# A hybrid encoder trunk: token norms spread by a trip through DRAM, mLSTM gates as 32 extra columns of the first value group

## The chip, the cores and the metric

The kernel runs on one core of one Trainium2 chip. The metric is device time in microseconds of one execution; lower is better. The core has five engines with in-order queues of their own: TensorE (PE in the profile; its weight loads are PEld), VectorE (DVE), ScalarE (ACT), GpSimd (POOL) and SyncE (SP), which here only issues DMAs.

## The reference

Two layers over 256 tokens of width 2048, everything in float32. What the change touches is the RMS norm ahead of every projection, and the gates of the second layer's mLSTM mixer:

```python
def rms_norm(x, g):
    y = xf * lax.rsqrt(jnp.mean(xf * xf, axis=-1, keepdims=True) + NORM_EPS)
    return (y * g)                       # one factor per token, one gain per channel
def mlstm_mixer(h, w_in, b_gate, h_norm, w_out):
    proj = h @ w_in                      # columns: q | k | v | o (2048 each) | 32 gates
    ...
    gates = proj[..., 4 * MLSTM_W:] + b_gate    # 4 kinds (i, f forward; i, f backward) x 8 heads
    h_fw = mlstm_one_direction(q, k, v, gates[0], gates[1])
    h_bw = flip(mlstm_one_direction(flip(q), flip(k), flip(v), flip(gates[2]), flip(gates[3])))
    ...                                  # sum, per-head norm, sigmoid output gate, output projection
for layer in range(2):
    h = rms_norm(x, norm_mix[layer])
    mixed = attention/pool mixer (layer 0) or mlstm_mixer (layer 1)
    x = x + mixed
    x = x + conv_ffn(rms_norm(x, norm_ffn[layer]), ...)
```

Inside a direction the forget gates are log-sigmoided and summed along the tokens, a running maximum is taken, and exp of both weighs a token-by-token matrix per head.

## The kernel before

**Precision and matmuls.** Each float32 operand is split in a high and a low part (type float32r), and a product is made of three matmuls: high x high, high x low, low x high. Weights stream from DRAM in chunks of 128 partitions x 1024 float32 (512 KB). `Stream` loads them on SP's queue into 6 buffers (`wraw`), and `split` makes the two parts: an ACT copy rounds to the high part (L87), a DVE subtraction leaves the low part (L88), into 4 buffers (`wsplit`). The split of a chunk is done two chunks ahead of its use.

**Two forms of a projection.** `stat_group` holds a weight block stationary and streams the 256 tokens (512 moving columns are the high and the low parts of the activations side by side, 256 the high ones alone); its output is channels x tokens. `mov_group` holds the activations stationary and streams weight columns; its output is tokens x channels, for each of 16 blocks of 128 input channels (`k`) 2 token halves x 3 matmuls of `width` columns. Both write tiles of the PSUM pool `mm`, which has two buffers; small products use the pool `ps` with four.

**Order.** TensorE's order is written out by hand: whatever the Python code emits first runs first (`manual_schedule`). ACT, DVE and POOL are ordered by the framework's scheduler, which follows readiness in a model of the time; an instruction without inputs can move far ahead. `Weave` puts side work between TensorE's main groups: each side task is a generator, a `yield d` asks to be continued when the estimated clock has moved on by d us, and that clock moves by `tick` after each `k` (0.645 in `stat_group`, 1.29 x width / 512 in `mov_group`). The emission, not the chip, follows this clock.

**Tiles.** A pool tile has a tag; tiles of one tag share the tag's buffers, and the framework makes a tile wait until a buffer is its own. The pool `t1p` (`ml_1`) of the mLSTM layer has one buffer a tag. Its tag `vf` holds in turn `wgf` (raw gate weights), `mvf0` (the scaled values of the first two heads, L804), `rows_a` (four rows of the gate work), and then `mvf1` and so on; `rows_b` takes the tag `at`.

**Norms.** `Norm.block` transposes the residual stream x on TensorE (`xt`), and `Norm.parts` gives gain and split (`xx`), without the per-token factor. `Norm.finish` adds up the squares, takes the inverse root (`rsqrt`, one POOL power and four small DVE steps), which gives `rcol`: tokens on partitions, 128 x 2. To have the same factors as a row on every partition, it builds two diagonal matrices `dg` (DVE, L270) and multiplies them with a matrix of ones on TensorE (`npr`), and copies the result to `R` (L275). `R` multiplies outputs that are channels x tokens: the pool channels, the FFN's up-projection (L850), mLSTM's q and k (L699). `rcol` scales outputs that are tokens x channels.

**mLSTM layer.** Per pair of heads: the values (`mov_group` of 512 columns, `mv0` to `mv3`), then q and k of each head (`stat_group`, `mq0`, `mk0`, ...), then the output gates (`mo`; for the last pair two groups of 256 columns). After `mv0` has been emitted its two halves are scaled into `mvf0` (ACT, L806) and split into `mvt0` (ACT L808, DVE L809). Then the task `gates` is added: on TensorE 16 x 2 stationary matmuls with gate weights padded to 104 rows (`gps`), emitted after the first `k` of `mq0`; then on ACT and DVE the chain that makes log-sigmoid (Abs, Exp, Ln: L665 to L667), sums (scans, L672 and L673), running maxima (L675 and L676), their sum (L677, the last use of `rows_a`) and an exp `E` (L678); the rows go to DRAM (`gd`), from where each head's `G` is spread to all partitions. 13.0 us of the estimated clock later TensorE transposes the maxima and `E` into columns (`cols`), which all heads need.

Of the kernel before, what the change touches and what calls it, by code (L numbers as in the profile page):

```python
# [9 lines left out]
F32 = mybir.dt.float32  # L10
F32R = mybir.dt.float32r
AF = mybir.ActivationFunctionType
# [4 lines left out]
P = 128  # L17
D = 2048
S = 256
KT = D // P  # L20
# [8 lines left out]
MH = 8  # L29
MD = 256  # L30
# [3 lines left out]
CH = 8  # L34
# [8 lines left out]


C_ID = 0
C_ONE = C_ID + P
C_CONV = C_ONE + P
C_PSC = C_CONV + 2 * 88 * 4
C_HN = C_PSC + 4
NC_ALL = C_HN + 16  # L50
# [14 lines left out]
class Stream:  # L65
# [6 lines left out]
        self.n_load = self.n_split = self.at = 0  # L72

    def load(self, pieces=1):
        i, n = self.n_load, CH * P // pieces
        w = self.wpool.tile([P, CH * P], F32, tag="w", name=f"w{i}")
        for c in range(0, CH * P, n):
            self.nc.sync.dma_start(w[:, c : c + n], self.srcs[i][:, c : c + n])
        self.w[i] = w, n
        self.n_load += 1  # L80

    def split(self):
        i = self.n_split
        w, n = self.w.pop(i)
        hl = self.spool.tile([P, 2, CH * P], F32R, tag="hl", name=f"hl{i}")
        for c in range(0, CH * P, n):
            self.nc.scalar.copy(hl[:, 0, c : c + n], w[:, c : c + n])  # L87
            self.nc.vector.tensor_sub(hl[:, 1, c : c + n], w[:, c : c + n], hl[:, 0, c : c + n].bitcast(F32))  # L88
        self.hl[i] = hl
        self.n_split += 1  # L90
# [60 lines left out]


@with_exitstack
def trunk(ctx: ExitStack, tc: tile.TileContext, xT, xn, gains, call, catt, cml, wgate, weights, out):
    nc = tc.nc
    v, a, g, pe = nc.vector, nc.scalar, nc.gpsimd, nc.tensor

    def pool(name, bufs, **kw):
        return ctx.enter_context(tc.tile_pool(name=name, bufs=bufs, **kw))
# [5 lines left out]
    sp = pool("wsplit", 4)  # L165
    smp = pool("small", 2)
    sm1 = pool("small1", 1)
    mmp = pool("mm", 2, space=PSUM)
    psp = pool("ps", 4, space=PSUM)

# [10 lines left out]

    wv = Weave()
    ident = cst[:, C_ID : C_ID + P]
    ones = cst[:, C_ONE : C_ONE + P]

    def gain(n, k):
        c = n * KT + k
# [2 lines left out]
    def mm(out_, lhsT, rhs, start, stop):  # L190
        pe.matmul(out_, lhsT, rhs, start=start, stop=stop, skip_group_check=True)  # L191
# [25 lines left out]
    class Norm:  # L217


        def __init__(self, n):  # L220
            self.n = n
            self.xx = actp.tile([P, KT, 2, S], F32R, tag="A", name=f"xx{n}")
            self.ss = smp.tile([P, 2, NB], F32, tag="nss", name=f"nss{n}")
            self.blocks, self.R = 0, None

        def at(self, k):

# [33 lines left out]
        def finish(self):  # L261
            n = self.n
            yield from wv.wait(lambda: self.blocks == NB)
            s2 = smp.tile([P, 2], F32, tag="nsum", name=f"nsum{n}")
            v.tensor_reduce(s2, self.ss, AX.X, ALU.add)
            self.rcol = rsqrt(s2, 2, 1.0 / D, f"n{n}")
            yield 2.5
            dg = sm1.tile([P, 2, P], F32, tag="dg", name=f"dg{n}")
            for t in range(2):
                v.tensor_scalar_mul(dg[:, t, :], ident, self.rcol[:, t : t + 1])  # L270
            yield 1.0
            pr = psp.tile([P, 512], F32, tag="ps", name=f"npr{n}")
            mm(pr[:, 0:S], ones, dg.rearrange("p a b -> p (a b)"), True, True)
            R = sm1.tile([P, S], F32, tag="R", name=f"R{n}")
            v.tensor_copy(R, pr[:, 0:S])  # L275
            self.R = R

    def stat_group(act, kts, name):
# [37 lines left out]

    def mov_group(act, name, width=512, before=None, after=None):

        ps = mmp.tile([P, 2, width], F32, tag="mm", name=name)
        per = CH * P // width  # L320
        hl = None
        for k in range(KT):
            if k % per == 0:
                before and before(k)
                hl = st.next()
                after and after(k)
            src = act(k)
            c = (k % per) * width
            for t in range(2):
                xh, xl = src[:, 0, t * P : t * P + P], src[:, 1, t * P : t * P + P]  # L330
                o = ps[:, t, :]
                first, last = k == 0 and (width == 512 or t == 0), k == KT - 1 and (width == 512 or t == 1)
                mm(o, xh, hl[:, 0, c : c + width], first, False)
                mm(o, xh, hl[:, 1, c : c + width], False, False)
                mm(o, xl, hl[:, 0, c : c + width], False, last)
            wv.tick(1.29 * width / 512)
        return ps
# [281 lines left out]
    def mlstm_layer(norm, nxt):  # L619
        with ExitStack() as es:  # L620
# [3 lines left out]
            kp, tp, t1p = lp("ml_c", 1), lp("ml_t", 2), lp("ml_1", 1)  # L624
            kc = kp.tile([P, NC_ML], F32, tag="kc", name="kml")
            a.dma_start(kc, cml)
            wgf = t1p.tile([P, KT, 4, MH], F32, tag="vf", name="wgf")
            a.dma_start(wgf.rearrange("p k c h -> p k (c h)"), wgate)

            wgp = actp.tile([P, KT, 2, P], F32R, tag="B0", name="wg")  # L630
            g.memset(wgp.bitcast(F32), 0.0)
            wg4 = wgp.rearrange("p k a (c h) -> p k a c h", c=4)[:, :, :, :, :MH]
            a.copy(wg4[:, :, 0], wgf)
            v.tensor_sub(wg4[:, :, 1], wgf, wg4[:, :, 0].bitcast(F32))
            wg = wgp[:, :, :, :NGATE]
            catb = [actp.tile([P, 8, 2, S], F32R, tag=f"B{i}", name=f"mcat{i}") for i in range(2)]

            def cat(k):
# [6 lines left out]
                [40, S], F32, tag="gd", name="gd")  # L645
            gate = []

            def gates():
                ps = psp.tile([P, 2, S], F32, tag="ps", name="gps")[:NGATE]
                for k in range(KT):  # L650
                    src = norm.xx[:, k]
                    mm(ps.rearrange("p a b -> p (a b)"), wg[:, k, 0, :], src.rearrange("p a b -> p (a b)"),
                       k == 0, False)
                    mm(ps[:, 1, :], wg[:, k, 1, :], src[:, 0, :], False, k == KT - 1)
                pre = kp.tile([NGATE, S], F32, tag="pre", name="pre")
                a.copy(pre, ps[:, 1, :])
                v.tensor_add(pre, ps[:, 0, :], pre)
                v.tensor_mul(pre, pre, norm.R[:NGATE])
                v.tensor_scalar_add(pre, pre, kc[:NGATE, M_BG : M_BG + 1])
                ra = t1p.tile([40, 4, S], F32, tag="vf", name="rows_a")  # L660
                rb = t1p.tile([40, 4, S], F32, tag="at", name="rows_b")
                la, le, ll, B, gg, M, E, on = (r[:, j, :] for r in (ra, rb) for j in range(4))
# [135 lines left out]
                    done.add(h)  # L798

            hns, done = {}, set()  # L800
            wv.add(norm.finish(), 8.0)
            for hp in range(MH // 2):
                ps = mov_group(xx, f"mv{hp}")
                vf = t1p.tile([P, 2, 512], F32, tag="vf", name=f"mvf{hp}")  # L804
                for t in range(2):
                    a.activation(vf[:, t, :], ps[:, t, :], AF.Copy, scale=norm.rcol[:, t : t + 1])  # L806
                vt = t1p.tile([P, 2, 2, 512], F32R, tag="vt", name=f"mvt{hp}")
                a.copy(vt[:, 0], vf)  # L808
                v.tensor_sub(vt[:, 1], vf, vt[:, 0].bitcast(F32))  # L809
                if hp == 0:  # L810
                    nrcol = kp.tile([P, 2], F32, tag="nrcol", name="nrcol")
                    v.tensor_scalar_mul(nrcol, norm.rcol, -1.0)
                    wv.add(gates())
                for hh in range(2):
                    h = 2 * hp + hh
                    q = scaled(stat_group(xx, list(range(KT)), f"mq{h}"), f"q{h}", MD ** -0.5)
                    kk = scaled(stat_group(xx, list(range(KT)), f"mk{h}"), f"k{h}", 1.0)
                    wv.add(head(h, q, kk, vt, hh))
                heads = [2 * hp, 2 * hp + 1]
                if hp < MH // 2 - 1:  # L820
                    wv.add(gated(mov_group(xx, f"mo{hp}"), heads))
                else:
                    for h in heads:
                        wv.add(gated(mov_group(xx, f"mo{hp}_{h}", MD), [h]))
# [95 lines left out]
def _stat(w, kts):  # L920

    k = len(kts)
    t = w.reshape(k, P, 2, P)[:, :, :, :]
    return t.reshape(k // 4, 4, P, 2, P).transpose(0, 2, 1, 3, 4).reshape(k // 4, P, CH * P)


def _mov(w):

    return w.reshape(-1, 2, P, 512).transpose(0, 2, 1, 3).reshape(-1, P, CH * P)
# [20 lines left out]
def _ml_chunks(w_in, w_out):  # L950
    a = []
    for hp in range(MH // 2):
        a.append(_mov(w_in[:, 2 * D + hp * 512 : 2 * D + hp * 512 + 512]))
        for h in (2 * hp, 2 * hp + 1):
            for part in (0, 1):
                c = part * D + h * MD
                a.append(_stat(w_in[:, c : c + 256], range(KT)))
        wo = w_in[:, 3 * D + hp * 512 : 3 * D + hp * 512 + 512]
        a += [_mov(wo)] if hp < MH // 2 - 1 else [_stat(wo[:, :MD], range(KT)), _stat(wo[:, MD:], range(KT))]
    return np.concatenate(a), _out_chunks(w_out, ML_PARTS)  # L960
# [123 lines left out]
```

## Time and profile before

| what | value |
|---|---|
| median of 3 runs | 2217.97 us (2217.95 to 2218.12) |
| the profiled execution | 2218.25 us, of which the profile's span is 2216.0 us |
| TensorE busy | 2205.2 us, 11650 matmuls |
| DVE / ACT / POOL busy | 1527.6 / 1169.5 / 33.4 us |
| granted TensorE clock | 1.0 (mean) |
| HBM traffic | 187 GB/s over the span |
| layer 0 mixer / FFN 0 / mLSTM mixer / FFN 1 begin | 0 / 263 / 997 / 1480 us |

A line of the page's fifth part names the code line, engine and operation, output and inputs, shapes and count, then busy time and the mean of one in ns, then the idle time of the engine just before and what ended it. The chain of the fourth part is followed back from the last instruction; its pieces in order of time give start, length, engine, tile, code line and count. TensorE's busy time by instruction overlaps (matmuls are pipelined), so the time of a group is read from the chain.

### The profile page before, as it was taken

What the parts mean: (1) busy time and instruction counts of PE and PEld (TensorE: products, weight loads), DVE (VectorE), ACT (ScalarE), POOL (GpSimd) and SP (SyncE); (2) the same over time, 40 slices, a digit from 0 to 9 for tenths busy, and PEclk for the clock granted to TensorE, in tenths of its full rate; (3) what the DMA queues carried; (4) which work ended last, traced back from release to release, by engine and by line L of the source; (5) the groups of instructions that cost most, each with busy time, mean ns of one, the idle gap of its engine ahead of it and who ended that gap; (6) DMA issues with size and microseconds to landing.
All of it is one profiled execution on the core that took longest, in us unless ns stands there. A gap on an engine that the chain in (4) does not pass through costs nothing.

```text
span 2216.0 us, 30515 instructions
## 1 busy us (share of the span) xinstructions
PE 2205.2 (100%) x11650; PEld 1887.1 (85%) x11650; DVE 1527.6 (69%) x2174; ACT 1169.5 (53%) x1662; POOL 33.4 (2%) x39
## 2 busy tenths in 40 slices
PE   8999999999999999999999999999999999999999
PEld 7888888888888888888888889888888888888887
DVE  7676677776676767666777676667777677676764
ACT  6665555554554545455554554455555455454542
POOL 1011000000000000000000000000000000000000
PEclk9999999999999999999999999999999999999999
DMA  8555566666666666654566555556656666666664
GB/s 317 167 165 163 177 190 189 191 190 192 190 191 190 191 191 189 196 188 156 178 193 186 180 183 171 184 178 190 190 190 190 190 190 191 190 190 190 190 191 141
DMA packets 117877, 415.45 MB, mean 187 GB/s; under 512 B 13115, under 2 KB 15587, under 8 KB 117731
## 3 DMA queue, kind: packets, MB, share of 16 engines
q1 hardware_dynamic: 114656, 410.02, 58.5%
q10 hardware_dynamic: 3074, 3.48, 0.7%
q8 instruction: 91, 1.49, 0.3%
q14 instruction: 56, 0.45, 0.1%
HBM read 411.31 MB, written 2.14 MB: 187 GB/s over the span
## 4 chain that ended last, share of the span: by engine, by line
PE 98%; ACT 1%; DVE 1%; DMA 0%; issue 0%; SPq 0%; DVEq 0%; ACTq 0%
PE up L191 44%; PE dn L191 21%; PE op L191 8%; PE mk L191 4%; PE mq L191 4%; PE mo L191 4%; PE mv L191 4%; PE qproj L191 3%; PE vproj L191 1%; PE kproj L191 1%; PE qk L191 1%; PE av L191 1%; PE end L191 1%; PE pool L191 0%; PE xt L242 0%; PE ov L191 0%
## 5 line engine op out<-in xcount | busy, mean ns | idle before, releaser
L88 DVE TENSOR_TENSOR hl<-w,hl 128x1024 fp32r<-128x1024 f32 (+1 forms) x769 | 937.7, 1220 | 470.7 <-ACT hl L87 469.1
L87 ACT CAST hl<-w 128x1024 fp32r<-128x1024 f32 (+1 forms) x769 | 806.7, 1050 | 683.7 <-PE dn L191 241.2
L191 PE MATMUL up<-xx,hl 128*128 128x512 f32 (+1 forms) x5632 | 984.2, 337 | 0.0
L191 PEld LDWEIGHTS up<-xx,hl 128*128 128x128 f32 x5632 | 857.9, 188 | 125.8
L191 PE MATMUL dn<-hl,g 128*128 128x512 f32 x2064 | 471.3, 389 | 0.0
L191 PEld LDWEIGHTS dn<-hl,g 128*128 128x128 f32 x2064 | 386.2, 188 | 79.5
L342 ACT COPY tb_up<-up 128x512 f32<-128x512 f32 x88 | 51.7, 587 | 154.0 <-PE up L191 154.0
L343 DVE TENSOR_TENSOR tb_up<-up,tb_up 128x512 f32<-128x512 f32 x88 | 60.9, 692 | 97.0 <-ACT tb_up L342 97.0
L854 ACT ACTIVATE y<-tb_up,cst 128x256 f32<-128x256 f32 x176 | 96.4, 595 | 46.9 <-DVE tb_up L850 46.9
L191 PE MATMUL mk<-xx,hl 128*128 128x512 f32 (+1 forms) x512 | 92.4, 338 | 0.0
L191 PE MATMUL mq<-xx,hl 128*128 128x512 f32 (+1 forms) x512 | 92.0, 337 | 0.0
L191 PE MATMUL op<-hl,cat 128*128 128x512 f32 x384 | 91.7, 393 | 0.0
L191 PE MATMUL mo<-hl,xx 128*128 128x512 f32 (+1 forms) x480 | 91.6, 348 | 0.0
L191 PE MATMUL mv<-hl,xx 128*128 128x512 f32 x384 | 89.6, 391 | 0.0
L191 PE MATMUL op<-hl,mcat 128*128 128x512 f32 x384 | 89.5, 392 | 0.0
L191 PEld LDWEIGHTS mq<-xx,hl 128*128 128x128 f32 x512 | 79.3, 188 | 11.7
L191 PEld LDWEIGHTS mk<-xx,hl 128*128 128x128 f32 x512 | 79.1, 188 | 11.4
L191 PEld LDWEIGHTS mo<-hl,xx 128*128 128x128 f32 x480 | 76.5, 190 | 10.6
L191 PEld LDWEIGHTS mv<-hl,xx 128*128 128x128 f32 x384 | 71.7, 188 | 14.8
L191 PEld LDWEIGHTS op<-hl,mcat 128*128 128x128 f32 x384 | 71.4, 188 | 14.6
L191 PEld LDWEIGHTS op<-hl,cat 128*128 128x128 f32 x384 | 70.9, 188 | 14.1
L857 DVE SCALAR_TENSOR_TENSOR y<-tb_up,cst,y 128x255 f32<-128x255 f32 x176 | 76.9, 479 | 0.0
(207 smaller groups left out, 1293.3 us busy)
## 6 DMA issues: line engine op xcount, KB each, us to landing
w<-in_up SPq DMA_DIRECT2D x352, 512.0 KB, 3.6
w<-in_dn SPq DMA_DIRECT2D x176, 512.0 KB, 4.0
w<-in_m_in SPq DMA_DIRECT2D x128, 512.0 KB, 3.6
w<-in_a_in SPq DMA_DIRECT2D x47, 512.0 KB, 4.1
w<-in_a_out SPq DMA_DIRECT2D x32, 512.0 KB, 3.4
w<-in_m_out SPq DMA_DIRECT2D x32, 512.0 KB, 3.4
xT<-in_xT SPq DMA_DIRECT2D x8, 256.0 KB, 6.9
x<-in_xn SPq DMA_DIRECT2D x4, 512.0 KB, 8.6
```

The lines of the kernel that those rows point to most:

```text
L87: self.nc.scalar.copy(hl[:, 0, c : c + n], w[:, c : c + n])
L88: self.nc.vector.tensor_sub(hl[:, 1, c : c + n], w[:, c : c + n], hl[:, 0, c : c + n].bitcast(F32))
L191: pe.matmul(out_, lhsT, rhs, start=start, stop=stop, skip_group_check=True)
L342: a.copy(tb, ps[:, :, 1, :])
L343: v.tensor_add(tb, ps[:, :, 0, :], tb)
L854: a.activation(y[:, j, :], u[:, j, :], AF.Identity, scale=cw(tl, 1), bias=cw(tl, 3))
L857: v.scalar_tensor_tensor(y[:, j, 0 : S - 1], u[:, j, 1:S], cw(tl, 2), y[:, j, 0 : S - 1], ALU.mult, ALU.add)
```

## The change

1. `Norm.finish` makes no `dg`, no `npr` and no copy. It writes `rcol` to a DRAM tile `rr` of 2 x 128 floats (a DMA on POOL's queue), and a second POOL DMA reads it back to all 128 partitions as `R`. The ones leave the constants (64 KB less to load).
2. The gate weights are no separate 256 KB load with padding, copy and split. Instead 32 gate columns stand behind the first head's 256 value columns: the first value group `mv0` becomes one group of 288 columns (six chunks of three `k`, the last with one) and one of 256 (four chunks).
3. `gates` starts after the group of 288 columns, one group earlier than the q projection where it started before. It scales the 32 columns by `rcol` into a zeroed tile `gn` (ACT), waits 3.0 us of the estimated clock, transposes it twice on TensorE into `gtr`, and adds the bias on DVE. What follows is as before, with the same tiles and tags.
4. `mvf0` is now taken before both groups and filled in two steps, one after each group.

The diff, without the lines that only follow from these (the constants' offsets, the arguments, the DRAM pool `nd`):

```diff
--- before.py
+++ after.py
...
         self.n_load = self.n_split = self.at = 0
 
     def load(self, pieces=1):
-        i, n = self.n_load, CH * P // pieces
+        i = self.n_load
+        width = self.srcs[i].shape[-1]
+        n = width // pieces
         w = self.wpool.tile([P, CH * P], F32, tag="w", name=f"w{i}")
-        for c in range(0, CH * P, n):
+        for c in range(0, width, n):
             self.nc.sync.dma_start(w[:, c : c + n], self.srcs[i][:, c : c + n])
-        self.w[i] = w, n
+        self.w[i] = w, n, width
         self.n_load += 1
 
     def split(self):
         i = self.n_split
-        w, n = self.w.pop(i)
+        w, n, width = self.w.pop(i)
         hl = self.spool.tile([P, 2, CH * P], F32R, tag="hl", name=f"hl{i}")
-        for c in range(0, CH * P, n):
+        for c in range(0, width, n):
             self.nc.scalar.copy(hl[:, 0, c : c + n], w[:, c : c + n])
             self.nc.vector.tensor_sub(hl[:, 1, c : c + n], w[:, c : c + n], hl[:, 0, c : c + n].bitcast(F32))
         self.hl[i] = hl
...
             v.tensor_reduce(s2, self.ss, AX.X, ALU.add)
             self.rcol = rsqrt(s2, 2, 1.0 / D, f"n{n}")
             yield 2.5
-            dg = sm1.tile([P, 2, P], F32, tag="dg", name=f"dg{n}")
-            for t in range(2):
-                v.tensor_scalar_mul(dg[:, t, :], ident, self.rcol[:, t : t + 1])
-            yield 1.0
-            pr = psp.tile([P, 512], F32, tag="ps", name=f"npr{n}")
-            mm(pr[:, 0:S], ones, dg.rearrange("p a b -> p (a b)"), True, True)
-            R = sm1.tile([P, S], F32, tag="R", name=f"R{n}")
-            v.tensor_copy(R, pr[:, 0:S])
+            rr = dram.tile([2, P], F32, tag="rr", name=f"rr{n}")
+            g.dma_start(rr.rearrange("t p -> p t"), self.rcol)
+            R = sm1.tile([P, 2, P], F32, tag="R", name=f"R{n}")
+            g.dma_start(R, rr.unsqueeze(0).to_broadcast([P, 2, P]))
+            R = R.rearrange("p t q -> p (t q)")
             self.R = R
 
     def stat_group(act, kts, name):
...
 
     def mov_group(act, name, width=512, before=None, after=None):
 
-        ps = mmp.tile([P, 2, width], F32, tag="mm", name=name)
+        ps = mmp.tile([P, 2, 512 if width > 256 else width], F32, tag="mm", name=name)
         per = CH * P // width
         hl = None
         for k in range(KT):
...
             c = (k % per) * width
             for t in range(2):
                 xh, xl = src[:, 0, t * P : t * P + P], src[:, 1, t * P : t * P + P]
-                o = ps[:, t, :]
-                first, last = k == 0 and (width == 512 or t == 0), k == KT - 1 and (width == 512 or t == 1)
+                o = ps[:, t, :width]
+                first, last = k == 0 and (width > 256 or t == 0), k == KT - 1 and (width > 256 or t == 1)
                 mm(o, xh, hl[:, 0, c : c + width], first, False)
                 mm(o, xh, hl[:, 1, c : c + width], False, False)
                 mm(o, xl, hl[:, 0, c : c + width], False, last)
...
             kp, tp, t1p = lp("ml_c", 1), lp("ml_t", 2), lp("ml_1", 1)
             kc = kp.tile([P, NC_ML], F32, tag="kc", name="kml")
             a.dma_start(kc, cml)
-            wgf = t1p.tile([P, KT, 4, MH], F32, tag="vf", name="wgf")
-            a.dma_start(wgf.rearrange("p k c h -> p k (c h)"), wgate)
-
-            wgp = actp.tile([P, KT, 2, P], F32R, tag="B0", name="wg")
-            g.memset(wgp.bitcast(F32), 0.0)
-            wg4 = wgp.rearrange("p k a (c h) -> p k a c h", c=4)[:, :, :, :, :MH]
-            a.copy(wg4[:, :, 0], wgf)
-            v.tensor_sub(wg4[:, :, 1], wgf, wg4[:, :, 0].bitcast(F32))
-            wg = wgp[:, :, :, :NGATE]
             catb = [actp.tile([P, 8, 2, S], F32R, tag=f"B{i}", name=f"mcat{i}") for i in range(2)]
 
             def cat(k):
...
                 [40, S], F32, tag="gd", name="gd")
             gate = []
 
-            def gates():
-                ps = psp.tile([P, 2, S], F32, tag="ps", name="gps")[:NGATE]
-                for k in range(KT):
-                    src = norm.xx[:, k]
-                    mm(ps.rearrange("p a b -> p (a b)"), wg[:, k, 0, :], src.rearrange("p a b -> p (a b)"),
-                       k == 0, False)
-                    mm(ps[:, 1, :], wg[:, k, 1, :], src[:, 0, :], False, k == KT - 1)
+            def gates(ps):
+
+                gn = t1p.tile([P, 2, P], F32, tag="arg", name="gn")
+                g.memset(gn, 0.0)
+                for t in range(2):
+                    a.activation(gn[:, t].rearrange("p (c h) -> p c h", c=4)[:, :, :MH],
+                                 ps[:, t, MD : MD + 32].rearrange("p (c h) -> p c h", c=4),
+                                 AF.Copy, scale=norm.rcol[:, t : t + 1])
+                yield 3.0
+                tr = psp.tile([P, S], F32, tag="ps", name="gtr")[:NGATE]
+                for t in range(2):
+                    pe.transpose(tr[:, t * P : t * P + P], gn[:, t, :NGATE], ident)
                 pre = kp.tile([NGATE, S], F32, tag="pre", name="pre")
-                a.copy(pre, ps[:, 1, :])
-                v.tensor_add(pre, ps[:, 0, :], pre)
-                v.tensor_mul(pre, pre, norm.R[:NGATE])
-                v.tensor_scalar_add(pre, pre, kc[:NGATE, M_BG : M_BG + 1])
+                v.tensor_scalar_add(pre, tr, kc[:NGATE, M_BG : M_BG + 1])
                 ra = t1p.tile([40, 4, S], F32, tag="vf", name="rows_a")
                 rb = t1p.tile([40, 4, S], F32, tag="at", name="rows_b")
                 la, le, ll, B, gg, M, E, on = (r[:, j, :] for r in (ra, rb) for j in range(4))
...
                     done.add(h)
 
             hns, done = {}, set()
-            wv.add(norm.finish(), 8.0)
+            wv.add(norm.finish(), 6.0)
             for hp in range(MH // 2):
-                ps = mov_group(xx, f"mv{hp}")
                 vf = t1p.tile([P, 2, 512], F32, tag="vf", name=f"mvf{hp}")
-                for t in range(2):
-                    a.activation(vf[:, t, :], ps[:, t, :], AF.Copy, scale=norm.rcol[:, t : t + 1])
+                for c, n in ((0, MD + 32), (MD, MD)) if hp == 0 else ((0, 512),):
+                    ps = mov_group(xx, f"mv{hp}_{c}", n)
+                    if hp + c == 0:
+                        wv.until(lambda: norm.rcol is not None)
+                        wv.add(gates(ps))
+                    n = min(n, 512 if hp else MD)
+                    for t in range(2):
+                        a.activation(vf[:, t, c : c + n], ps[:, t, :n], AF.Copy, scale=norm.rcol[:, t : t + 1])
                 vt = t1p.tile([P, 2, 2, 512], F32R, tag="vt", name=f"mvt{hp}")
                 a.copy(vt[:, 0], vf)
                 v.tensor_sub(vt[:, 1], vf, vt[:, 0].bitcast(F32))
                 if hp == 0:
                     nrcol = kp.tile([P, 2], F32, tag="nrcol", name="nrcol")
                     v.tensor_scalar_mul(nrcol, norm.rcol, -1.0)
-                    wv.add(gates())
                 for hh in range(2):
                     h = 2 * hp + hh
                     q = scaled(stat_group(xx, list(range(KT)), f"mq{h}"), f"q{h}", MD ** -0.5)
...
 def _ml_chunks(w_in, w_out):
     a = []
     for hp in range(MH // 2):
-        a.append(_mov(w_in[:, 2 * D + hp * 512 : 2 * D + hp * 512 + 512]))
+        c = 2 * D + hp * 512
+        a.append(_mov(w_in[:, c : c + 512]) if hp else _stat(w_in[:, c + MD : c + 512], range(KT)))
         for h in (2 * hp, 2 * hp + 1):
             for part in (0, 1):
                 c = part * D + h * MD
...
     bgate = np.zeros((2, 2, 32), f32)
     bgate[:, :, :MH] = i["b_gate_c"][0].reshape(2, 2, MH).transpose(1, 0, 2)
     cml = np.concatenate([masks, bgate.reshape(P, 1)], axis=1)
+
     wgate = i["w_in_c"][0][:, 4 * D :].reshape(KT, P, 2, 2, MH).transpose(1, 0, 3, 2, 4).reshape(P, KT, 32)
+    wv0 = i["w_in_c"][0][:, 2 * D : 2 * D + MD].reshape(KT, P, MD).transpose(1, 0, 2)
+    m_g = np.concatenate([wv0, wgate], axis=2).reshape(P, KT * (MD + 32))
     a_in, a_out = _att_chunks(i["w_in_ab"][0], i["w_out_ab"][0])
     m_in, m_out = _ml_chunks(i["w_in_c"][0], i["w_out_c"][0])
     arrays = {
         "xT": i["x"][0].T.reshape(KT, P, S).transpose(1, 0, 2), "gains": gains,
         "xn": i["x"][0].reshape(2, P, D).transpose(1, 0, 2),
-        "call": call, "catt": catt, "cml": cml, "wgate": wgate,
+        "call": call, "catt": catt, "cml": cml, "m_g": m_g,
         "a_in": a_in, "a_out": a_out, "m_in": m_in, "m_out": m_out,
     }
     for l in range(2):
...
         u, d = chunks(f"up{l}"), chunks(f"dn{l}")
         return [(u if w == "u" else d)[j] for w, j in _ffn_order()]
 
-    weights = chunks("a_in") + chunks("a_out") + ffn(0) + chunks("m_in") + chunks("m_out") + ffn(1)
+    n = 3 * (MD + 32)
+    vg = [t["m_g"][:, c : min(c + n, m_g.shape[1])] for c in range(0, m_g.shape[1], n)]
+    weights = chunks("a_in") + chunks("a_out") + ffn(0) + vg + chunks("m_in") + chunks("m_out") + ffn(1)
     with tile.TileContext(nc, schedule_with_timeline_sim=True) as tc:
-        trunk(tc, t["xT"], t["xn"], t["gains"], t["call"], t["catt"], t["cml"], t["wgate"], weights, o)
+        trunk(tc, t["xT"], t["xn"], t["gains"], t["call"], t["catt"], t["cml"], weights, o)
     r = _run(nc, [{f"in_{k}": val for k, val in arrays.items()}], core_ids=[0])
     y = r.results[0]["out"]
     return np.ascontiguousarray(y.transpose(1, 0, 2)).reshape(1, S, D)
```

More of the change, by code (lines that the diff above doesn't have):

```diff
@@ L45 @@
 C_ID = 0
-C_ONE = C_ID + P
-C_CONV = C_ONE + P
+C_CONV = C_ID + P
 C_PSC = C_CONV + 2 * 88 * 4
@@ L153, in trunk @@
 @with_exitstack
-def trunk(ctx: ExitStack, tc: tile.TileContext, xT, xn, gains, call, catt, cml, wgate, weights, out):
+def trunk(ctx: ExitStack, tc: tile.TileContext, xT, xn, gains, call, catt, cml, weights, out):
     nc = tc.nc
@@ L167, in trunk @@
     sm1 = pool("small1", 1)
+    dram = pool("nd", 2, space=bass.MemoryType.DRAM)
     mmp = pool("mm", 2, space=PSUM)
@@ L183, in trunk @@
     ident = cst[:, C_ID : C_ID + P]
-    ones = cst[:, C_ONE : C_ONE + P]
     def gain(n, k):
@@ L223, in __init__ @@
             self.ss = smp.tile([P, 2, NB], F32, tag="nss", name=f"nss{n}")
-            self.blocks, self.R = 0, None
+            self.blocks, self.R, self.rcol = 0, None, None
         def at(self, k):
@@ L1033 @@
     call = np.concatenate(
-        [np.eye(P, dtype=f32), np.ones((P, P), f32)] + conv
+        [np.eye(P, dtype=f32)] + conv
         + [per_part(i["pool_scale"][0]), per_part(i["h_norm_c"][0])], axis=1)
```

## The prediction

> **What bounds the kernel.** I read the chain that ended last first, by engine and then in order of time around the mLSTM layer.
>
> ```profile
> PE 98%; ACT 1%; DVE 1%; DMA 0%; issue 0%; SPq 0%; DVEq 0%; ACTq 0%
> ```
>
> ```profile
> 1003.85 8.20 PE mv L191 x36
> 1012.48 8.21 PE mv L191 x36
> 1021.38 5.55 PE gps L191 x32
> 1026.92 10.46 PE mq L191 x60
> ...
> 1362.71 7.19 PE mo L191 x60
> ...
> 1438.12 1.39 PE op L191 x6
> 1439.94 1.39 PE op L191 x6
> ```
>
> TensorE never stops between these pieces, so a matmul taken out is worth its own time, and a stop in it is paid in full. Prices: a 512-column matmul 8.21/36 = 0.228 us; a 256-column one 7.19/60 = 0.120 us; one `k` of a stationary group 4 x 10.46/60 = 0.697 us. The hole between the two `op` pieces (1439.51 to 1439.94) is four transposes, 0.108 us each; that between the two `mv` pieces (1012.05 to 1012.48) is `npr`, 0.43 us.
>
> The other view is the timeline after the value group (start, length, engine, line), because the change moves the gate chain against it.
>
> ```profile
> 1020.73 1.26 ACT L806 ACTIVATE mvf<-mv,re_n 128x512 f32<-128x512 f32 x2 [1.67 <-PE mv L191]
> ...
> 1024.10 1.22 DVE L809 TENSOR_TENSOR mvt<-mvf,mvt 128x1024 fp32r<-128x1024 f32 x1
> 1025.43 0.27 DVE L670 MEMSET rows_a<- 40x256 f32 x1
> ...
> 1030.05 0.41 ACT L665 ACTIVATE rows_a<-rows_b 40x256 f32<-40x256 f32 x1
> ...
> 1039.01 0.41 DVE L677 TENSOR_TENSOR rows_b<-rows_a,rows_b 40x256 f32<-40x256 f32 x1
> ...
> 1040.99 0.42 ACT L678 ACTIVATE rows_b<-rows_b 40x256 f32<-40x256 f32 x1
> ...
> 1041.50 1.08 PE L191 MATMUL cols<-cst,rows_b 40*128 40x40 f32 x8
> ```
>
> ```profile
> L669 DVE MEMSET rows_b<- x1: 272/272/272, 196.4 to 196.4; 40x256 f32 x1
> ```
>
> Two things stand here. `E` is done at 1041.41 and `cols` starts at 1041.50: today's 13.0 us of estimated clock just covers the chain. And the memset of `rows_b`, which has no inputs, ran at 196 us, as early as its memory was there; that of `rows_a`, equally without inputs, ran at 1025.43, 0.1 us after the last reader of `mvf0` (L809, done at 1025.32), though the tag's earlier tile (`wgf`) was done by 957 and DVE had idle time. So tiles of tag `vf` take the one buffer in the order of the code, and `rows_a` waits until `mvf0` is finished with.
>
> **The change, part by part.**
>
> *TensorE's work.* Gone: `gps`, 5.55 us, and four `npr`, 4 x 0.43 = 1.72. The value group was 96 x 0.228 = 21.9 us; now 96 matmuls of 288 columns and 96 of 256. On the line through the two prices (0.108 us for 256 more columns) 288 columns take 0.133 us, so 12.8 + 11.5 = 24.3, or 2.4 more. Bounds for the unseen width: 0.120 (1.1 more in all) and 0.228 (11.5 more); I take 0.133, as 256 and 512 lie on one line through nearly nothing at 0. Added: two transposes, 0.22. Sum: -5.55 - 1.72 + 2.4 + 0.2 = -4.65 us.
>
> *The gate chain: the term that decides.* Call T1 the end of the 256-column group. `gates` is added before that group and takes its second step after the sixth of its `k` (5 x 0.645 = 3.2 us of estimated clock past the first). There it emits the two transposes and the whole chain; 13.0 later, after ten more `k` of this group (6.45) and eleven of `mq0` (7.1), `cols` is emitted. On TensorE `cols` therefore stands at T1 + 11 x 0.697 = T1 + 7.7 us. But `rows_a` must have the buffer of `mvf0`, and `mvf0` is now taken before both groups and filled and split only after the second: scaling, rounding, subtraction come after T1, as before. Before, that took from 1020.69 (end of `mv0`) to 1025.32, 4.6 us; half the scaling is gone, so 4.3. From the first use of `rows_a` (L665, 1030.05) to `E` (1041.41) the chain took 11.36 us. `E` is then ready at T1 + 4.3 + 11.4 = T1 + 15.7, and TensorE stands still from 7.7 to 15.7: 8.0 us. Before, `gates` began after `mq0`'s first `k`, and `mvf0` was gone (1025.3) before the chain wanted the buffer (1028.7), so this wait did not exist. Bounds: without the weight split that sits in the chain (1.2 us of DVE at 1035.8) and without the one ahead of L808 (1.1), 5.7 us; with one more split ahead of the chain, 9.4.
>
> *The clock behind the stop.* No stop of this length is in the trace; the nearest rows are its two ends.
>
> ```profile
> 2214.00:2215.00 1.00, 0.00 (x0) 0.00 (x0) 0.00 (x0) 0.00 (x0) 0.00 (x0) 0.77 0.38 131
> 2215.00:2216.00 1.00, 0.00 (x0) 0.00 (x0) 0.00 (x0) 0.00 (x0) 0.00 (x0) 0.50 0.00 0
> ```
>
> (Of the last three columns the first is the granted clock; DMA share and GB/s follow.) The last matmul ended at 2212.2; the clock had gone to a half some 2.5 us later. At the start ten passes of 128x256 (`wps`, 4.63 us) took 0.46 us each where `npr` takes 0.43/2 = 0.215, so a cold engine runs at half speed for 4 to 5 us. Half of that is lost: 2.0 us, with 0 and 2.6 as ends. The Trainium skill (TensorE: Matmul & The Clock Gate, Part 1) says that the clock halves after an idle window of about 3.4 us and comes back after as long of steady work; by that page the loss would be 1.7 and the sum 0.3 us lower. The trace's ends agree in kind.
>
> *R through DRAM.* `rcol` is there at 1486.1 in FFN 1, and L850 wants `R` at 1493.8, or 1493.4 without `npr` ahead of it: 7.3 us (FFN 0 the same: 269.6 and 277.3). No POOL DMA is in the trace. The nearest rows, on ACT's queue: the write of `gd` let the next DMA go 1.7 us after it was issued; a 128 KB spread of `G` lands after 3.0 to 6.6 us, 5.0 in the middle; issuing takes 0.3 to 0.7. Twice issue, write, read: 5.3 to 9.7, I take 8, so L850 waits 1 us or 2. Behind it on DVE stand the weight splits (L88 at 1494.44). A split is cast once its buffer comes free and is needed three chunks (3 x 2.79 us) later, so that one, done at 1495.66, is needed near 1500.6: 5 us of cover, and L850 may wait as long for nothing. Cost 0. In layer 0 POOL's queue behind the two DMAs holds the power for k (41.5), which TensorE needs at 56.4 with rows ending at 49.7; in the mLSTM layer `R` is first wanted a whole q group after. Both have over 6 us of cover. The diagonals (0.28 us each) leave DVE, also in the crowded stretch at 33 us; there the split behind them waits for ACT in any case. The Trainium skill (DMA: Bandwidth & Descriptors, Rules for kernel authors) speaks against the write: a scattered last dimension becomes one descriptor per element, here 256 of 4 bytes. It gives no time for so few, and no row shows one; it is weighed below.
>
> *Loads and splits.* 8 chunks become 10 with 6% more columns; POOL's zeroing of `wg` (3.5 us), one ACT copy and one DVE subtraction near 955 go. All of it lies in idle time of those engines. The smallest chunk (0.8 us of TensorE) shortens the lead of a split from 8.2 to 5.6 us, against about 2.3 that it takes. Cost 0.
>
> **Sum.** 2218.25 (the profiled execution: span 2216.0 and 2.25 around it) - 4.65 + 8.0 + 2.0 = 2223.6. The median lies 0.28 lower: 2223.3. With the ends of the stop and of the clock this case reaches from 2219.0 (5.7 and 0) to 2225.3 (9.4 and 2.6).
>
> **Rivals.**
> 1. *No stop: the chain does not wait for `mvf0`* (its buffer is handed on otherwise than I read it, say). The chain could then start at the transposes, 4.3 us into the group of 256, and `E` would come at about T1 + 5, before 7.7. Only TensorE's sum is left: 2217.97 - 4.65 = 2213.3, faster. Against it: the 1025.43 memset. Point of decision: `mvf0` released by T1 - 3.7.
> 2. *`rows_a` takes the buffer before `mvf0`.* Then the scaling of `mvf0` waits for L677, about 15.5 us after the end of the 288 group, T1 + 3.8; `mq0` needs that group's PSUM buffer and starts at T1 + 4.8. Stop 4.8 and clock 2.0: 2217.97 - 4.65 + 6.8 = 2220.1. The same memset speaks against it.
> 3. *R late.* If the two hops take over 12.3 us after `rcol` (7.3 + 5), the splits run out in both FFNs. At 16 us each, 3.7 + 3.7 on top of the forecast: 2230.7. For it: the scattered write; against it: 9.7 us as the upper end.
> 4. *288 columns at the price of 512*: 9.1 more on TensorE, 2232; against it, the line through the two widths.
>
> **Chances.** Forecast 0.64, rival 1 0.22, rival 2 0.08, rivals 3 and 4 together 0.06. A measurement of this kernel tells about 0.2% (4.4 us) from no change. Rival 1 lies on that edge (4.65): 0.14 faster, 0.08 same. The forecast, +5.3, has about a quarter of its spread under +4.4: 0.16 same, 0.48 slower. Rival 2 is the same, 3 and 4 slower. Faster 0.14, same 0.32, slower 0.54. The range goes from rival 1 to a little past the forecast's upper end, 2213.0 to 2226.5; the forecast's own is 2219.0 to 2225.3.
>
> **What would show it.** In the profile after: `cols` with a wait of 8 us on ACT `E` (L678's successor) eleven `k` into `mq0`; the first use of `rows_a` right after the subtraction of `mvt0`; a granted clock of a half behind the stop; no `npr`, no `gps`; the groups of value columns at 12.8 and 11.5 us; L850 waiting under 5 us in each FFN with TensorE unbroken. Wrong would be a TensorE chain without that stop (rival 1), or with one at the start of `mq0` (rival 2), or `up` matmuls waiting on L88 (rival 3).

## The result and the profile after

The changed kernel takes 2230.35 us (median of 6 runs, 2229.81 to 2231.78) and the kernel before 2217.98 (6 runs, 2217.92 to 2218.12) on the same chip: ratio 1.0056 [1.0045, 1.0068], 12.4 us slower. The forecast was 2223.3: the sign is right, the time lies outside the range. The profiled execution after took 2229.94 us, its span is 2228.1 (before 2216.0).

The first matmuls of `up` and of `mv` divide the span into four stages. This table (us, from the timelines of the profiled executions) locates the differences.

| kernel | layer-0 mixer | FFN 0 | mLSTM mixer | FFN 1 and end | span |
|---|---|---|---|---|---|
| before | 263.30 | 734.04 | 482.47 | 736.19 | 2216.0 |
| after | 263.02 | 737.96 | 489.85 | 737.27 | 2228.1 |
| e1 norm rows alone | 264.11 | 737.83 | 481.99 | 737.67 | 2221.6 |
| e2 gates alone | 263.29 | 734.04 | 489.50 | 736.17 | 2223.0 |
| e3 after, `rows_a` in a buffer of its own | 262.89 | 737.60 | 479.02 | 736.99 | 2216.5 |
| e4 gates alone, `rows_a` in its own | 263.87 | 734.04 | 479.46 | 736.13 | 2213.5 |
| e6 as e3, norms written as rows | 262.96 | 733.72 | 479.13 | 735.89 | 2211.7 |

So the loss is 7.4 us in the mLSTM mixer, 3.9 in FFN 0 and 1.1 in FFN 1. The chain that ended last, by engine, shows DMA with a share that it did not have:

```profile
PE 96%; DMA 1%; DVE 1%; ACT 1%; issue 0%; SPq 0%; DVEq 0%; ACTq 0%; POOLq 0%
```

TensorE's waits (engine, line, waited for: us in total, times, longest) name the two places, the gate columns and the weight splits of `up`:

```profile
PE cols L192 <- DVE rows_b L667: 5.4, 1, 5.4
PE up L192 <- DVE hl L89: 3.7, 2, 2.5
PE cols L192 <- ACT rows_b L669: 1.6, 1, 1.6
```

**The first place.** The same chain in order of time, around the value group:

```profile
1001.14 3.96 PE mv L192 x30
...
1006.77 12.24 PE mv L192 x96
1019.01 0.22 PE gtr L648 x2
1019.23 7.20 PE mv L192 x60
...
1029.41 1.23 DVE mvt L805
1030.64 0.02 issue
1030.66 0.42 ACT rows_a L656
...
1041.61 0.42 ACT rows_b L669
1042.03 0.04 issue
1042.07 1.07 PE cols L192 x4
1043.15 6.48 PE mq L192 x20
1049.63 11.14 PE mk L192 x64
```

T1, the end of the 256-column group, is 1019.23 + 7.20 = 1026.43. The first use of `rows_a` (L656) stands right behind the subtraction of `mvt0` (L805), which is the last reader of `mvf0`. `E` (L669) is done at 1042.03. TensorE meanwhile worked through 44 matmuls of `mq0` until 1034.09, then stood but for four of the eight `cols`. The end of `cols` is at 1043.14: 9.05 us, of which `cols` itself takes 1.01. Stop: 8.0 us.

Behind it, 20 matmuls of `mq` take 6.48 us; at 0.697/4 = 0.174 each they would take 3.48. The windows (stretch, length, PE, PEld, DVE, ACT and POOL busy, granted clock, DMA share, GB/s) show why:

```profile
1039.00:1042.00 3.00, 1.07 (x4) 0.93 (x4) 1.01 (x3) 1.68 (x2) 0.00 (x0) 0.50 0.46 172
1043.00:1045.00 2.00, 2.00 (x7) 1.63 (x7) 0.68 (x8) 0.24 (x1) 0.00 (x0) 0.50 0.29 88
1047.00:1049.00 2.00, 2.00 (x8) 1.71 (x7) 0.99 (x3) 0.00 (x0) 0.00 (x0) 0.50 0.32 80
1049.00:1051.00 2.00, 2.00 (x12) 1.74 (x12) 0.69 (x1) 1.33 (x2) 0.00 (x0) 0.94 0.58 198
288.00:290.00 2.00, 2.00 (x8) 1.76 (x8) 1.64 (x3) 1.99 (x3) 0.00 (x0) 0.51 0.54 209
290.00:292.00 2.00, 2.00 (x9) 1.66 (x9) 1.56 (x3) 2.00 (x4) 0.00 (x0) 0.63 0.82 246
1511.00:1513.00 2.00, 0.86 (x5) 0.42 (x3) 1.78 (x3) 1.05 (x3) 0.00 (x0) 1.00 0.00 0
1513.00:1515.00 2.00, 1.90 (x11) 1.73 (x12) 2.00 (x6) 1.67 (x3) 0.00 (x0) 1.00 0.44 123
1515.00:1517.00 2.00, 2.00 (x13) 1.72 (x13) 1.19 (x3) 1.99 (x4) 0.00 (x0) 1.00 0.67 170
```

The clock is at a half from 1039.0 to 1049.2, so 3.0 us more are lost after work has resumed.

**The second place.** The chain at the start of FFN 0, and the two DMAs in the list of issues (KB each, median us from issue to landing):

```profile
269.63 8.75 DMA rr<-re_n
...
278.94 5.64 DMA R<-rr
...
285.28 1.23 DVE hl L89
286.51 0.04 issue
286.55 13.45 PE up L192 x67
```

```profile
R<-rr POOLq DMA_DIRECT2D x4, 128.0 KB, 6.1
rr<-re_n POOLq DMA_DIRECT2D x4, 1.0 KB, 8.6
```

The write of 1 KB takes longer than the read of 128 KB that follows. `R` is there at 284.58, 14.95 us after the write was issued; DVE, with the splits queued behind L845, starts the next one at 285.28, and TensorE has run out of split weights 2.49 us before it resumes at 286.55. In FFN 1 `R` takes 13.69 us (1497.44 to 1511.13) and TensorE stops for 1.24. The windows above add what follows: after the stop of 2.49 us the clock is at a half from 288.06 to 291.47; after that of 1.24 us it stays at 1.00.

### The profile page after: what moved, and what is told of

Read it like the earlier page. It is cut to its first block, busy times and chain, and to the rows that moved or that the text cites. A ratio compares the mean times of both kernels' runs of the same rounds, so it can differ in the third digit from the quotient of the medians.

```text
span 2228.1 us, 30646 instructions
## 1 busy us (share of the span) xinstructions
PE 2206.2 (99%) x11708; PEld 1891.2 (85%) x11708; DVE 1522.6 (68%) x2161; ACT 1170.1 (53%) x1666; POOL 31.6 (1%) x47
## 4 chain that ended last, share of the span: by engine, by line
PE 96%; DMA 1%; DVE 1%; ACT 1%; issue 0%; SPq 0%; DVEq 0%; ACTq 0%; POOLq 0%
PE up L192 43%; PE dn L192 21%; PE op L192 8%; PE mv L192 4%; PE mk L192 4%; PE mo L192 4%; PE mq L192 4%; PE qproj L192 2%; PE vproj L192 1%; PE pool L192 1%; PE kproj L192 1%; DMA rr<-re_n 1%; PE qk L192 1%; PE av L192 1%; DVE hl L89 1%; PE end L192 1%
## 5 line engine op out<-in xcount | busy, mean ns | idle before, releaser
L849 ACT ACTIVATE y<-tb_up,cst 128x256 f32<-128x256 f32 x176 | 96.4, 595 | 64.0 <-DVE tb_up L845 64.0
L192 PE MATMUL mv<-hl,xx 128*128 128x512 f32 (+2 forms) x480 | 91.7, 350 | 0.0
L192 PEld LDWEIGHTS mv<-hl,xx 128*128 128x128 f32 x480 | 78.3, 188 | 11.2
```

Source lines behind the costliest of these rows:

```text
L849: a.activation(y[:, j, :], u[:, j, :], AF.Identity, scale=cw(tl, 1), bias=cw(tl, 3))
```

## The experiments

Theory A is the forecast's stop in the mLSTM layer, plus a late `R` in both FFNs. The first four kernels separate the two parts and remove the buffer from the first; the rest ask why the write is slow and what cures it.

**e1, the norm rows alone.** The kernel before with this in `finish`:

```diff
-dg = sm1.tile([P, 2, P], F32, tag="dg", name=f"dg{n}")
...
-mm(pr[:, 0:S], ones, dg.rearrange("p a b -> p (a b)"), True, True)
-R = sm1.tile([P, S], F32, tag="R", name=f"R{n}")
-v.tensor_copy(R, pr[:, 0:S])
+rr = dram.tile([2, P], F32, tag="rr", name=f"rr{n}")
+g.dma_start(rr.rearrange("t p -> p t"), self.rcol)
+R = sm1.tile([P, 2, P], F32, tag="R", name=f"R{n}")
+g.dma_start(R, rr.unsqueeze(0).to_broadcast([P, 2, P]))
+R = R.rearrange("p t q -> p (t q)")
```

> The kernel before with the norm rows alone passed through DRAM on POOL's queue; gates, value group and tiles as before. Theory A (two separate stops: R lands some 14 to 15 us after rcol, 12.4 us of cover, so TensorE stops in both FFNs): +3.9 us in FFN 0, +1.1 in FFN 1, about -0.4 in each mixer, so 2222.2 us, slower by 4.3, with up waiting for L88's DVE split in both FFNs. Theory C (the late R is a by-product of the new gates and of what they shift): no stop in the FFNs, four times 0.43 us saved, 2216.3.

Measured 2223.01 us (11 runs) against 2218.30: 1.0022 [1.0013, 1.0031]. FFN 0 is 3.8 us longer and FFN 1 1.5, the mLSTM mixer 0.5 shorter (its `npr`). The layer-0 mixer is 0.8 longer in the profiled execution, for a reason told under e7. The wait is that of the whole change:

```profile
PE up L192 <- DVE hl L88: 3.9, 2, 2.4
```

So the norm rows alone make the kernel slower, though they take 1.72 us off TensorE.

**e2, the gates alone.** The changed kernel with `dg`, `npr` and the copy back in `finish`.

> The changed kernel with the norm rows made on TensorE again (diagonals, ones, npr); the gates as in the change. Theory A: the mLSTM mixer loses what it lost in the change, 7.4 us, and 0.4 for its npr: 2225.8, with cols stopped for about 8 us and a half clock behind it, and FFNs as before. Theory C': the mLSTM stop comes from the POOL DMAs of the norm: no stop, 2215.0.

Measured 2225.43 us (5 runs): 1.0034 [1.0021, 1.0047]. The mLSTM mixer is 7.0 us longer, both FFNs are as before to 0.02 us, and both waits of `cols` (5.4 and 1.6) are there. The two parts hardly touch each other: 4.7 + 7.1 = 11.8, against 12.4 for the whole.

**e3, `rows_a` in a buffer of its own.** The changed kernel with one word altered; tag `og` is not in use at this time.

```diff
-ra = t1p.tile([40, 4, S], F32, tag="vf", name="rows_a")
+ra = t1p.tile([40, 4, S], F32, tag="og", name="rows_a")
```

> The changed kernel with one tag changed: rows_a takes the buffer of og, idle at that time, and no longer that of mvf0. Theory A (the chain waits for mvf0's buffer): the 8.0 us stop at cols and about 3.0 us of half clock go, 2230.35 - 11.0 = 2219.3, with the FFN stops left. Theory B (the chain is late because ACT and DVE split the second half of mvf0 then, whatever the buffer): cols still stops for 5 us or more, 2227 to 2230.

Measured 2217.84 us (11 runs) against 2218.30: 1.0000 [0.9991, 1.0008]. The chain at the same place:

```profile
1018.74 7.19 PE mv L192 x60
1025.93 7.66 PE mq L192 x44
1033.59 1.01 PE cols L192 x8
1034.60 3.69 PE mq L192 x20
```

All eight `cols` run in one piece, at T1 + 7.66, and the 20 matmuls behind them take 3.69 us in place of 6.48. The mLSTM mixer falls by 10.8 us (489.85 to 479.02), 8.0 + 3.0 by the reading above; the FFNs keep their loss. That the buffer made the stop is shown.

**e4, gates alone with `rows_a` in its own buffer** (e2 with e3's edit).

> The changed gates with rows_a in the buffer of og, and the norm rows on TensorE as before. Theory A: no stop at all, only TensorE's work differs: -5.55 (gps) + 2.4 (288 + 256 columns for 512) + 0.2 (two transposes) = -2.95, 2215.0, faster than before. Theory B: 2222 to 2226.

Measured 2215.12 us (11 runs) against 2218.30: 0.9985 [0.9977, 0.9994]. The mixer gains 3.01 us. The memset of `rows_a` shows the rule of the tags once more: with its buffer free, it runs at 197 us, where `rows_b`'s was.

```profile
L665 DVE MEMSET rows_a<- x1: 272/272/272, 197.2 to 197.2; 40x256 f32 x1
```

**e5 and e9, what makes the write slow.** The kernel before, with a chain of small writes and reads back added behind each norm; each waits for the one ahead. Their times say nothing. All but two carry the same 256 numbers (1 KB) and differ in where the pieces lie; `dd` and `dz` write whole rows of 256 and 64 bytes.

```diff
+da = dram.tile([2, P], F32, tag="da", name=f"da{n}")
+g.dma_start(da.rearrange("t p -> p t"), self.rcol)
+g.dma_start(rb[0], da.rearrange("t p -> p t"))
+db = dram.tile([P, 2], F32, tag="db", name=f"db{n}")
+g.dma_start(db, rb[0])
...
+dc = dram.tile([2, P, 16], F32, tag="dc", name=f"dc{n}")
+g.dma_start(dc[:, :, 0].rearrange("t p -> p t"), rb[1])
...
+a.dma_start(de.rearrange("t p -> p t"), rb[3])
```

`da` is the change's own write, 256 pieces of 4 bytes side by side; `db` 128 pieces of 8 bytes side by side; `dc` 256 pieces of 4 bytes, each 64 bytes from the next; `dd` [P, 64], rows; `de` is `da` from ACT's queue. In e9 `dz` is [P, 16], rows; `dy` and `dx` are as `dc`, 32 and 16 bytes apart; `da` comes last.

> The kernel before, with five writes to DRAM and a read back of each added after every rcol, one after the other; nothing uses what is read, so the kernel's time says nothing. da: 256 elements of 4 bytes scattered, POOL's queue (as in the change); db: 128 rows of 8 bytes, POOL; dc: 256 elements, each on 64 bytes of its own, POOL; dd: 128 rows of 256 bytes, POOL; de: as da, from ACT's queue. Theory S (small elements that share a 64-byte line are written one after the other): da and de 7 to 9 us from issue to landing, db 4 to 6, dc and dd 2 to 3. Theory N (the number of elements): da, dc and de 7 to 9, db 4 to 6, dd 2 to 5. Theory Q (POOL's queue is slow for every DMA): da to dd all 6 to 9, de 2 to 3.

> A second probe on the kernel before, in the other order, on POOL's queue after every rcol; nothing uses what is read, so the kernel's time says nothing. dz: 128 rows of 64 bytes; dy: 256 elements of 4 bytes, 32 bytes apart (2 to a 64-byte line); dx: 16 bytes apart (4 to a line); da: side by side (16 to a line), last in the chain this time. If elements that share a line are written one after the other: dz about 2 us, dy 2 to 4, dx 3 to 5, da 8 to 10, and the reads back follow in the same order (rba 6). If it was the place in the chain (the first writes meet more weight traffic): dz slowest, da 2 to 4.

Measured in one execution each, four writes of each kind (issues of e5, then of e9; the lines `rb..` are the reads back; the last number is the median):

```profile
dd<-wide POOLq DMA_DIRECT2D x4, 32.0 KB, 1.7
da<-re_n POOLq DMA_DIRECT2D x4, 1.0 KB, 9.3
rba<-da POOLq DMA_DIRECT2D x4, 1.0 KB, 6.1
db<-rba POOLq DMA_DIRECT2D x4, 1.0 KB, 7.0
...
dc<-rbb POOLq DMA_DIRECT2D x4, 1.0 KB, 2.0
rbc<-dc POOLq DMA_DIRECT2D x4, 1.0 KB, 2.1
...
de<-rbd ACTq DMA_DIRECT2D x4, 1.0 KB, 10.5
```

```profile
dz<-wide POOLq DMA_DIRECT2D x4, 8.0 KB, 2.3
...
dy<-rba POOLq DMA_DIRECT2D x4, 1.0 KB, 3.8
...
dx<-rbb POOLq DMA_DIRECT2D x4, 1.0 KB, 3.8
...
da<-rbc POOLq DMA_DIRECT2D x4, 1.0 KB, 10.4
```

Neither the number of pieces nor the queue decides: `dc` has as many 4-byte pieces as `da` and lands in 2.0 us, and ACT's queue is no faster than POOL's. What decides is that small pieces lie close together: 256 pieces of 4 bytes within 1 KB take 9.3 to 10.5 us, within 4 or 8 KB 3.8, within 16 KB 2.0. (The step from 3.8 to 2.0 lies between two executions, and rows read back also took 3.4 in e9 and 1.9 in e5, so that step alone is not shown.) Its place in the chain does not matter either (first 9.3, last 10.4). The pieces themselves move early: in the changed kernel the packets of POOL's queue run from 271.06 to 271.93, while the write counts as done at 278.38. Why closeness costs the rest was not tried further, and stays open.

**e6, the norms turned into rows first.** e3's edit, and a transpose by TensorE ahead of the write, so that it has two pieces of 512 bytes:

```diff
-yield 2.5
+yield 1.5
+trow = psp.tile([P, 512], F32, tag="ps", name=f"nrow{n}")[:2, :P]
+pe.transpose(trow, self.rcol, ident)
+row = sm1.tile([2, P], F32, tag="row", name=f"row{n}")
+v.tensor_copy(row, trow)
 rr = dram.tile([2, P], F32, tag="rr", name=f"rr{n}")
-g.dma_start(rr.rearrange("t p -> p t"), self.rcol)
+g.dma_start(rr, row)
```

> The changed kernel with rows_a in the buffer of og, and rcol turned on TensorE (one transpose of 128 x 2, 0.1 us), copied to two rows of 512 bytes and written so to DRAM; R is read back as in the change. If the scattered elements make the write slow (S or N): the write lands in 2 to 4 us, R about 12 us after rcol with the wait for TensorE's turn, within the 12.4 us of cover: no stop in the FFNs or one under 1 us, 2213.9 to 2215.5. If POOL's queue is slow for every DMA (Q): R is later than in the change, 2218 to 2221.

Measured 2213.81 us (11 runs) against 2218.53: 0.9979 [0.9970, 0.9988], 4.7 us faster than before and 16.5 faster than the change as it was made. The write lands in 3.3 us, the read in 4.5:

```profile
R<-rr POOLq DMA_DIRECT2D x4, 128.0 KB, 4.5
...
rr<-row POOLq DMA_DIRECT2D x4, 1.0 KB, 3.3
```

and at the start of FFN 0 the chain is TensorE's alone:

```profile
268.18 2.81 PE up L192 x16
270.99 0.11 PE nrow L270
271.10 29.04 PE up L192 x166
```

L849 (L845 of the changed kernel) runs at 281.19, 11.6 us after the norms at 269.6, and DVE waits 3.07 us for `R`; TensorE sees nothing of it. FFN 0 is 733.72, 0.32 under the kernel before, which is `npr` (0.43) less the transpose (0.11).

**e7, DRAM rows for the two mixer norms only** (scattered as in the change, `npr` for the FFN norms; `rows_a` in its own buffer), to take the gain where `R` is not urgent.

```diff
+if n % 2 == 0:
+    rr = dram.tile([2, P], F32, tag="rr", name=f"rr{n}")
+    g.dma_start(rr.rearrange("t p -> p t"), self.rcol)
...
+    return
 dg = sm1.tile([P, 2, P], F32, tag="dg", name=f"dg{n}")
```

> rows_a in the buffer of og; norm rows through DRAM for the two mixers alone, where R is wanted late, and on TensorE for the two FFNs. Theory A: 2215.1 (the version with all four on TensorE) - 2 x 0.43 = 2214.3, no stop in the FFNs. Rival: POOL's wait for the write holds back the q and k powers of layer 0, and the gain goes there: 2215.1 or more.

Measured 2215.19 us (11 runs) against 2218.53: 0.9985 [0.9976, 0.9994], no better than e4. The mLSTM mixer takes the expected 0.44 (479.46 to 479.02), but in the profiled execution, which took 2217.01 us, the layer-0 mixer grows by 1.5 (263.87 to 265.36). Its clock shows why:

```profile
8.36:11.77 3.41, 1.80 (x7) 0.95 (x6) 2.56 (x5) 2.84 (x5) 0.00 (x0) 1.00 1.02 406
11.77:15.18 3.41, 3.41 (x10) 2.67 (x9) 3.29 (x6) 3.26 (x7) 0.00 (x0) 0.50 1.04 410
```

3.41 us at half the clock, with TensorE busy, are 1.7 us lost, and they lie ahead of the first write to `rr` at 33.47, so the edit did not bring them. The two waits ahead (0.85 and 0.76 us) stand in e4 as well, at the full clock. The extra 0.8 us in the layer-0 mixers of e1 and e10 is of the same kind: their clock is at a half from 36.43 to 39.85 and from 36.29 to 39.70, behind two waits (1.13 and 0.76 us) that the kernel before has too. Another wait is in every kernel whose layer-0 norm passes through DRAM (after, e1, e3, e6, e7, e10) and in none of the others:

```profile
PE ov L194 <- DVE pt L489: 1.2, 1, 1.2
```

Why it comes was not settled. After, e3 and e6 have it with a layer-0 mixer of 262.89 to 263.02, less than the 263.30 before, so it does not cost what it shows. Why e7's median shows nothing of the expected 0.86 us stays open; it is less than the executions of one kernel differ by.

**e8, `cols` later instead of another buffer** (e2, `rows_a` still in `mvf0`'s buffer):

```diff
-yield 13.0
+yield 21.0
```

> The changed gates with rows_a in mvf0's buffer as in the change, the norm rows on TensorE, and cols emitted 21.0 us of the estimated clock after the chain in place of 13.0 (12 k of 0.697 us = 8.4 us later on TensorE). Theory A: the chain still waits for mvf0 and ends 15.7 us after the value groups, but TensorE meets cols only at 16.0: no stop, 2215.0 to 2216. If heads or the wait for G turn late instead: over 2218.

Measured 2216.68 us (11 runs) against 2218.53: 0.9995 [0.9986, 1.0004]. `cols` now waits 0.7 us on `E` instead of 7.0, and the mLSTM mixer is 480.34, 9.2 less than in e2 and 0.9 more than in e4. The buffer still holds the chain up, but TensorE has other work meanwhile.

**e10, the row write in the kernel before** (old gates, e6's rows).

> The kernel before with its gates, and the norm rows turned on TensorE, written to DRAM as two rows of 512 bytes and spread from there. If the scattered write alone made part 1 of the change slow: no stop in the FFNs, and four times 0.43 - 0.11 us saved on TensorE: 2218.3 - 1.3 = 2217.0. If the trip through DRAM itself is too slow: 2219 to 2222.

Measured 2217.67 us (11 runs) against 2218.28: 0.9996 [0.9987, 1.0005]. No stop in either FFN (each 0.3 shorter); the layer-0 mixer is 0.8 longer in the profiled execution, with the stretch of half clock told under e7. By the median the norm rows are worth 0.6 us when they are in time, which the interval does not tell from nothing; from e4 to e6 they are worth 1.3 (2215.12 to 2213.81), and TensorE's own work is 1.28 less.

## Why the prediction was right and wrong

*TensorE's work: right.* The 288-column matmuls run at 3.96/30 = 0.132 us (forecast 0.133). With the stops cured and `npr` kept, e4's mixer gains 3.01 us, where these terms give 5.55 - 2.4 - 0.2 = 2.95. With the rows in time, e6's span is 4.3 below the span before, where they give 4.65 less four transposes (0.44).

*The gate chain: right.* `E` came at T1 + 15.6 (forecast 15.7), `cols` stood ready at T1 + 7.7, the stop was 8.0. Rival 1 and rival 2 are ruled out by the chain and by e3: the memset at 1025.43 was read rightly.

*The clock behind the stop: right in kind, too small.* 3.0 us in place of 2.0, over the upper end of 2.6. The half clock lasted 10.24 us, from 1039.0 to 1049.2, and 6.1 of that lay on working matmuls, not the 4 to 5 seen at the start of the kernel. The Trainium skill (TensorE: Matmul & The Clock Gate, Part 1: The HAM clock gate) says that the gate watches a window of 3413 ns that runs on by itself. Both lengths in this trace agree: 3.41 us in FFN 0, and 10.24, which is three times that. So do their places: they begin 750.9 us apart (288.06 and 1038.99), which is 220 such windows. The Trainium skill's drop after about 3.4 idle us is not what FFN 0 shows, where a stop of 2.49 us was enough and the drop came 1.5 us after work had resumed.

*R through DRAM: the step that failed.* "Twice issue, write, read: 5.3 to 9.7, I take 8" became 14.95 and 13.69. The term mis-sized is the write: 1.7 us from `gd`, which is 40 KB in whole rows, measured at 8.6 for 1 KB in 256 pieces. With it falls the step behind it, "L850 may wait as long for nothing. Cost 0". The read (6.1) lay inside its bounds of 3.0 to 6.6. The cover was right: 14.95 - 2.49 = 12.46 and 13.69 - 1.24 = 12.45 us, forecast 12.3. So rival 3's condition was met in addition to the forecast's stop, with a price of 2.49 + 1.24, and about 1.9 of half clock in FFN 0 that no step had foreseen (what is left of 3.92 + 0.43 for `npr` behind the stop; half of the 3.41 us is 1.7). These 5.6 us alone lead out of the range; without them the sum ends inside it, near 2224.6. That rival 3's own figure, 2230.7, lies so near the measured time is in part luck: it put `R` at 16 us in both FFNs, later than it came, and left out the half clock in FFN 0. Its chance was too small because the bound from `gd` was taken as if a write's price hung on the bytes; how the pieces lie, which the prediction itself names, was left out of the range.

The sum with the measured terms: 2218.25 - 4.65 + 8.0 + 3.0 + (2.49 + 1.9) + 1.24 = 2230.2, the profiled execution being 2229.94.

*Loads and splits: right,* no wait of TensorE on them is new but those behind `R`.

## What to carry to other kernels

A tile that shares a one-buffer tag waits for its neighbour in the order of the code: when a producer is moved ahead, look which buffer its first tile takes and who reads that last. One word (another tag) was worth 10.8 us here, and the change turns from slower to faster with it and with a write in rows.

A column spread over 128 partitions is turned on TensorE (0.11 us) before it goes to DRAM, if anybody waits for it. A DMA that has no near row in the trace deserves a range that reaches the point at which its cover ends, and not the price of a write of another form.

## What the runs showed of the hardware that was not expected

256 pieces of 4 bytes written side by side into 1 KB of DRAM are done only after 8.6 to 10.5 us, on either queue; 128 pieces of 8 bytes after 7.0, two rows of 512 bytes after 3.3, and 256 pieces 64 bytes apart after 2.0. Reading them back costs 6.1 against 2.1 us. The Trainium skill (DMA: Bandwidth & Descriptors, Anatomy of one DMA — SWDGE (gpsimd) path) puts a DMA's fixed cost at about 2 us, most of it the wait for the receipt of the last byte: the writes in rows or 64 bytes apart agree with 1.7 to 3.3, those side by side do not.

Stops of TensorE shorter than one stretch of half clock (3.41 us) brought such a stretch: 2.49, 2.36 and 2.19 us in FFN 0 of after, e1 and e3, where the stops of FFN 1 in the same three, 1.24, 1.59 and 0.94 us, did not. The place counts too. Within a trace the stretches begin a whole number of 3.413 us apart (220 in after, 74 in e1), and the same two waits, 1.13 and 0.76 us, brought one in e1 and e10 and none in the kernel before. Read off these traces, and not tested by an experiment: cut at these places, the 3.41 us ahead of each drop held 1.6 us or more of idle time in all, added over the waits. So what a short stop costs depends in part on where it happens to fall, and a single profiled execution can be off by the 1.7 us of one such stretch.
